# Gate and up projections as 15 products of three weight rows, two width halves and three token groups

## The chip, the core and the metric

The kernel runs on one core of a Trainium2 chip. The metric is device time in microseconds (us) from the start of the program to its end; lower is better. Five engines work side by side, each through its own queue in order: PE multiplies matrices, DVE and ACT work on tiles (both can read PE's result banks), POOL works on tiles that lie in SBUF, and SP here only issues transfers (DMAs) between DRAM and SBUF. An engine that waits for another holds up whatever stands behind the waiting instruction in its queue.

## What is computed

One layer of a decoder for 1024 prompt tokens and 32 sampled tokens, so 1056 in all, with a width of 1024 and a hidden width of 2816:

```python
def _layer(x, p, attn_fn, ...):
    h = _rms(x, n_mix_pre)
    z = h @ w_in
    ...
    mix = jnp.concatenate([a, m], axis=-1) @ w_out
    x = x + _rms(mix, n_mix_post)
    f = _rms(x, n_ffn_pre)
    f = (jax.nn.silu(f @ w_gate) * (f @ w_up)) @ w_down
    x = x + _rms(f, n_ffn_post)
    x = x + jax.nn.sigmoid(x @ w_ple_gate) * (p @ w_ple)
```

The change concerns `f @ w_gate`, `f @ w_up` and, for one third of the tokens, `@ w_down`.

## The kernel before

**Tokens and operands.** The 1056 tokens are three groups of N = 352 columns, numbered 0, 1, 2. Features lie on the 128 partitions. Every float32 operand of a matmul is kept as two parts, a rounded high part and the rest: `split` (L166) makes them with a copy on ACT and a subtraction on DVE. A product of 128 x 128 weights with 352 columns is then three matmuls (`gemm`, L412: high by high, high by low, low by high). A weight row of a block is 128 x 1024; over half of the width (four pieces of 128) a product costs 12 matmuls, over all of it 24.

**Gate and up.** The hidden width is 22 blocks of 128; each has a gate row and an up row. Groups 0 and 1 use a seven-product scheme: gate and up are two rows, the width has two halves (1 and 2), the groups are two columns, and the 2 x 2 x 2 product is made with seven half-width products instead of eight, from sums of weights and sums of operands (`T1` to `T4`, L1046). `w_sums` (L1122) forms the four weight sums with four POOL additions of 128 x 512, and splits them. Group 2 is done directly with the plain rows (`direct`, L1161). `gate_up` (L1151) runs one block: 7 x 12 + 2 x 24 = 132 matmuls. Its additions of product banks to SBUF tiles run on DVE.

**Order.** The blocks go in pairs, called slabs, 11 of them. `WALK` (L214) sets the order: first five slabs for group 2 alone, while the norms of groups 0 and 1 are still under way on the other engines, then all 11 for groups 0 and 1, six of them with group 2 as well. The down product of group 2 (`down`, L1215) is spread between the blocks: eight banks a slab, added to a running sum. PE's instructions stand in program order; those of the other engines are placed by a scheduler. `chain` and `turn` (L383) feed the steps of the norms (`ffn_steps`, L1002) in between, paced by a number of matmuls.

**Weights.** `need(k)` (L341) prepares the weights of item k and of up to four items behind it: it loads them into one of three raw buffers (`W_RAW`), and splits them into one of four pairs of buffers (`W_PAIRS`).

**Behind it.** The hidden rows of groups 0 and 1 and their differences are split at once (`stage`, L1082), written to DRAM with both parts (`spill`), and read back (`x_get`, L1259) for the down product in the same seven-product form (`down7`, L1271). Then the closing part (`ple_steps`, `ple_out`, `ple_first`, `ple_rest`) follows.

## Time and profile before

| | |
|---|---|
| three timed runs | 1077.48, 1078.29 (median), 1081.69 us |
| profiled execution | span 1076.7 us; no time of its own is listed beside it |
| HBM read, written | 123.02 MB, 37.86 MB |
| weight rows of gate and up read | 64 transfers of 512 KB |
| splits of plain weight rows (DVE, L168, `wl`) | 123, 162.9 us |
| weight sums on POOL (L1132, `wr`) | 47 + 46, 69.1 + 65.0 us |
| sums for the down stage on POOL (L339) | 44, 77.4 us |

In the profile's groups a row gives line, engine, operation, written tile <- read tiles, shapes, count; then busy time in us and the mean of one instruction in ns; then the idle time of the engine just ahead of them and what ended it. Names have their buffer numbers left out: `b` is a bank of PE's results, `wr` a raw weight row, `wh` and `wl` its two parts.

### The profile page before, as it was taken

The page shows a single profiled execution, that of the slowest core. Times are in us where ns is not written, and L with a number is a line of the kernel's source. Part 1 is how long each engine was busy: PE and PEld are TensorE (multiplying, and loading weights), DVE is VectorE, ACT ScalarE, POOL GpSimd, SP SyncE. Part 2 cuts the span into 40 slices and gives each one's busy share as a digit, 9 for nine tenths or more (in the row PEclk, how much of TensorE's full clock was granted, in tenths as well). Part 3 has the DMA queues.
Part 4 walks back from the last instruction along what each step waited for, and adds up shares of the span by engine and source line. Part 5 has one row for each costly group of instructions (what it writes and reads, how often), then busy time and mean ns, then how long its engine had stood idle before and what let it go on. Part 6 is the DMA issues. An engine that isn't in the chain of part 4 may idle for free.

```text
span 1076.7 us, 17467 instructions
## 1 busy us (share of the span) xinstructions
PE 1065.5 (99%) x6805; PEld 1049.6 (97%) x6805; DVE 828.7 (77%) x1229; ACT 525.7 (49%) x951; POOL 285.5 (27%) x213
## 2 busy tenths in 40 slices
PE   9999999999999999999999999999999999999997
PEld 8999988899999999999999999999999999999997
DVE  6766378977979957767758758659668877999898
ACT  8522277776855524344434434434344832476542
POOL 1045022200000032422324223232309076401170
PEclk9999999999999999999999999999999999999999
DMA  8121311352644312352441533614876955836422
GB/s 299 60 72 40 108 54 37 136 217 90 228 154 134 109 40 81 144 186 71 159 168 59 212 114 107 236 43 160 310 267 230 405 189 181 310 114 216 138 67 74
DMA packets 54162, 162.01 MB, mean 150 GB/s; under 512 B 5796, under 2 KB 20164, under 8 KB 54080
## 3 DMA queue, kind: packets, MB, share of 16 engines
q1 hardware_dynamic: 52752, 159.13, 42.2%
q10 hardware_dynamic: 1328, 1.77, 0.5%
q8 instruction: 53, 0.87, 0.4%
q14 instruction: 29, 0.24, 0.1%
HBM read 123.02 MB, written 37.86 MB: 149 GB/s over the span
## 4 chain that ended last, share of the span: by engine, by line
PE 91%; DVE 5%; ACT 2%; issue 1%; DMA 0%; ACTq 0%; SPq 0%; DVEq 0%
PE b L126 90%; DVE sl L168 1%; DVE sg L1439 1%; PE b L120 1%; DVE u L1286 1%; DVE ql L168 1%; DVE yo L1440 1%; DVE p L1476 0%; DMA xr<-in_x_dram 0%; ACT a L780 0%; DVE w L168 0%; DVE acc L930 0%; ACT qh L167 0%; DVE u L1476 0%; ACT sg L1436 0%
## 5 line engine op out<-in xcount | busy, mean ns | idle before, releaser
L126 PE MATMUL b<-fh,wh 128*128 128x352 f32 x720 | 231.4, 322 | 0.0
L126 PE MATMUL b<-fl,wh 128*128 128x352 f32 x716 | 229.3, 320 | 0.0
L126 PE MATMUL b<-fh,wl 128*128 128x352 f32 x716 | 229.2, 320 | 0.0
L1132 POOL TENSOR_TENSOR wr<-wr 128x512 f32<-128x512 f32 x47 | 69.1, 1470 | 538.1 <-DVE wl L168 512.4
L168 DVE TENSOR_TENSOR wl<-wr,wh 128x1024 fp32r<-128x1024 f32 (+1 forms) x123 | 162.9, 1326 | 51.3 <-ACT wh L167 51.2
L167 ACT CAST wh<-wr 128x1024 fp32r<-128x1024 f32 (+1 forms) x123 | 126.1, 1027 | 123.1 <-PE b L126 96.5
L126 PE MATMUL b<-xo,qh 128*128 128x352 f32 x620 | 147.7, 321 | 0.5 <-ACT u L1314 0.5
L126 PEld LDWEIGHTS b<-fh,wh 128*128 128x128 f32 x720 | 134.9, 188 | 0.0
L126 PE MATMUL b<-fh,sh 128*128 128x352 f32 x420 | 134.6, 322 | 0.0
L126 PEld LDWEIGHTS b<-fl,wh 128*128 128x128 f32 x716 | 134.5, 188 | 0.0
L126 PE MATMUL b<-fh,sl 128*128 128x352 f32 x416 | 133.2, 320 | 0.9 <-DVE sl L168 0.9
L126 PEld LDWEIGHTS b<-fh,wl 128*128 128x128 f32 x716 | 134.1, 187 | 0.0
L126 PE MATMUL b<-fl,sh 128*128 128x352 f32 x416 | 133.2, 320 | 0.0
L126 PE MATMUL b<-h,wh 128*128 128x352 f32 x480 | 112.6, 325 | 1.4 <-ACT h L504 1.2
L126 PEld LDWEIGHTS b<-xo,qh 128*128 128x128 f32 x620 | 107.1, 188 | 0.7 <-ACT u L1314 0.7
L126 PE MATMUL b<-xo,ql 128*128 128x352 f32 x308 | 99.1, 322 | 1.4 <-DVE ql L168 1.2
L339 POOL TENSOR_TENSOR wq<-wq,wq 128x512 f32<-128x512 f32 x44 | 77.4, 1797 | 66.0 <-DVE ql L168 56.3
L167 ACT CAST st<-c 128x352 fp32r<-128x352 f32 x55 | 26.8, 487 | 122.8 <-DVE c L1201 96.6
L126 PEld LDWEIGHTS b<-h,wh 128*128 128x128 f32 x480 | 83.3, 190 | 2.5 <-ACT h L504 1.4
L168 DVE TENSOR_TENSOR sl<-wr,sh 128x1024 fp32r<-128x1024 f32 x47 | 59.5, 1266 | 33.1 <-ACT sh L167 33.1
L126 PE MATMUL b<-hid,wh 128*128 128x352 f32 x352 | 84.0, 321 | 0.0
L126 PEld LDWEIGHTS b<-fh,sl 128*128 128x128 f32 x416 | 77.9, 187 | 1.2 <-DVE sl L168 1.2
(211 smaller groups left out, 2177.8 us busy)
## 6 DMA issues: line engine op xcount, KB each, us to landing
wr<-in_w_gu_dram SPq DMA_DIRECT2D x64, 512.0 KB, 3.4
xd<-st SPq DMA_DIRECT2D x35, 704.0 KB, 4.9
xo<-xd SPq DMA_DIRECT2D x35, 704.0 KB, 6.1
wr<-in_w_dn_dram SPq DMA_DIRECT2D x22, 512.0 KB, 4.2
wq<-in_w_dn_dram SPq DMA_DIRECT2D x20, 512.0 KB, 9.6
wr<-in_w_pg_dram SPq DMA_DIRECT2D x10, 512.0 KB, 3.5
x<-in_x_dram SPq DMA_DIRECT2D x6, 704.0 KB, 9.1
x1d<-x SPq DMA_DIRECT2D x6, 704.0 KB, 3.3
```

Of the source, the lines that this page charges most:

```text
L120: ins = te.transpose(out, src, ident)
L126: ins = te.matmul(*args, **kw)
L167: fix(se.copy(hi, src))
L168: fix(ve.tensor_tensor(lo, src, hi.bitcast(F32), op=ALU.subtract))
L339: ge.tensor_tensor(*(q_load(q, e)[:, i, :] for q in (out, a, b)), op=op)
L1132: ge.tensor_tensor(out, a, b, op=op)
L1286: ve.tensor_tensor(out, a, b, op=ALU.add)
L1439: ve.tensor_tensor(sg[:, v], sg[:, v], pp[:, v], op=ALU.mult)
L1440: ve.tensor_tensor(yo[:, v], sg[:, v], xm[:, v], op=ALU.add)
```

## The change

Gate and up use another scheme, with 15 half-width products for three weight rows, two halves and three groups, where the plain form has 18. The 44 rows form 14 triples (gate and up of one block, and one row of another) and a last pair with 11 products. Four of the 15 products of a triple need only the first two rows. They are made ahead, for all triples, in two passes (`two_ahead`), and written to DRAM (`p_d`), as are two half-row sums of weights (`s_d`). Then each triple loads both, and runs its 11 remaining products from six weight forms called 5, 3, 10, 8, 9 and 15 (`w_form`, `triple`). Form 9 is the last to read the first two rows. Some of the sums of pre-products run on POOL (`part_sums`). The hidden rows go to DRAM unsplit, half the bytes, and are split when they are read back (`x_get`, `hid_split`). The down product of group 2 becomes one block behind all triples (`down2`), with its eight banks held through it. Raw weight buffers are four instead of three.

```diff
-W_RAW = 3
+W_RAW = 4
+ROWS = 13
...
+    for t, rows in enumerate(TRIPLES):
+        FORM[t, "one"] = item("one", row_plan(*rows[0]), t)
+    for t, rows in enumerate(TRIPLES):
+        FORM[t, "two"] = item("two", row_plan(*rows[1]), t)
+    for t, rows in enumerate(TRIPLES):
+        jr = [row_plan(*r) for r in rows]
+        js = add_plan(s_d[t], [P, KC, P])
+        in_a.add(js)
+        FORM[t, "5"] = item("5", *jr[:2])
+        FORM[t, "3"] = item("3", js, *jr[:2])
+        FORM[t, "10"] = item("10", js, *jr[2:])
+        if len(rows) > 2:
+            FORM[t, "8"] = item("8", jr[2])
+        FORM[t, "9"] = item("9", *jr)
+        if len(rows) > 2:
+            FORM[t, "15"] = item("15", js, jr[2])
...
+        if kind in ("one", "two"):
+            r = raws[js[0]]
+            at = slice(4, 8) if kind == "one" else slice(0, 4)
+            add(r[:, at, :], r[:, 0:4, :], r[:, 4:8, :])
+            nc.sync.dma_start(s_d[js[1]][:, at, :], r[:, at, :])
+            hl = w_tile([P, KC, P], "fh"), w_tile([P, KC, P], "fl")
+            split(*hl, r)
+            return hl
...
+        if kind == "5":
+            r0, r1 = r
+            add(r0[:, one, :], r0[:, one, :], r1[:, two, :], sub)
+            split(*hl, r0[:, one, :])
+        elif kind == "3":
+            s, r0, r1 = r
+            add(r0[:, one, :], r0[:, one, :], s[:, one, :])
+            add(r1[:, two, :], r0[:, two, :], r1[:, two, :])
+            halves(r0[:, one, :], r1[:, two, :])
+        elif kind == "10":
+            if len(r) > 1:
+                add(r[0], r[0], r[1])
+            split(*hl, r[0])
+        elif kind == "8":
+            split(*hl, r[0])
+        elif kind == "9":
+            if len(r) > 2:
+                add(r[1][:, one, :], r[1][:, one, :], r[2][:, one, :])
+                add(r[0][:, two, :], r[0][:, two, :], r[2][:, two, :])
+            halves(r[1][:, one, :], r[0][:, two, :])
+        else:
+            s, r2 = r
+            add(s[:, one, :], s[:, one, :], r2[:, two, :])
+            add(s[:, two, :], s[:, two, :], r2[:, one, :])
+            split(*hl, s)
...
+    def two_ahead(t, i):
+
+        w = need(FORM[t, ("one", "two")[i]])
+        st = act_tile([P, 2, N], s="st")
+        for h, key in enumerate((("X1", "B23"), ("B11", "X4"))[i]):
+            at = 1 - h if i else h
+            se.copy(st[:, at, :], product(w, h, key)[:, :N])
+        nc.sync.dma_start(p_d[t][:, 2 * i : 2 * i + 2, :], st)
...
+    def part_load(t):
+        if t < NT:
+            parts[t] = [act_tile([P, 4, N], s="p")]
+            nc.sync.dma_start(parts[t][0], p_d[t])
+
+    def part_sums(t):
+        if t < NT:
+            p = parts[t][0]
+            q = act_tile([P, 4, N], s="q")
+            parts[t].append(q)
+            ge.tensor_tensor(q[:, 0:2, :], p[:, 0:2, :], p[:, 1:3, :], op=ALU.add)
+            ge.tensor_tensor(q[:, 2, :], p[:, 0, :], p[:, 3, :], op=ALU.add)
+            ge.tensor_tensor(q[:, 3, :], p[:, 2, :], p[:, 3, :], op=ALU.add)
...
+        part_load(t + 1)
+        b5 = product(need(FORM[t, "5"]), None, "X5")
+        tt(q2, b5[:, :N], q2)
+        w3 = need(FORM[t, "3"])
+        b3 = product(w3, 0, "X3")
+        tt(q2, b3[:, :N], q2, sub)
+        w = need(FORM[t, "10"])
+        b10 = product(w, 0, "X10")
+        if full:
+            tt(p3, b10[:, :N], p3)
+        b13 = product(w, 1, "X13")
+        if full:
+            tt(p1, b13[:, :N], p1)
+        product(w3, 1, "X6", b5)
+        tt(q1, b5[:, :N], q1, sub)
+        se.activation(q[:, 0:2, :], q[:, 0:2, :], AF.Silu)
+        if full:
+            w = need(FORM[t, "8"])
+            b8 = product(w, 0, "B12")
+            c32 = tmp(N, "c32")
+            se.copy(c32, b8[:, :N])
+            tt(p2, b8[:, :N], p2)
+            b11 = product(w, 1, "B22")
+            tt(p0, b11[:, :N], p0)
+            tt(c32, b11[:, :N], c32)
+        part_sums(t + 1)
+        tt(q[:, 0:2, :], q[:, 0:2, :], q[:, 2:4, :], ALU.mult)
+        w = need(FORM[t, "9"])
+        product(w, 0, "X9", b10)
+        tt(p2, b10[:, :N], p2, sub)
+        product(w, 1, "X12", b13)
+        tt(p0, b13[:, :N], p0, sub)
+        h1 = tmp(N, "h1")
+        se.activation(h1, p0, AF.Silu)
+        tt(h1, h1, p2, ALU.mult)
+        c = rows[0][0]
+        chunk_put(c, q1, h1, q0)
++        if not full:
             return
+        w = need(FORM[t, "15"])
+        product(w, 0, "X15", b11)
+        minus(p3, b11, p3)
+        product(w, 1, "X14", b8)
+        minus(p1, b8, p1)
...
+    def down2():
+
+        os_[2] = [half(2, s="o") for h in range(2)]
+        banks = [bank() for _ in range(KC)]
+        for s in range(NSLAB):
+            hid_get(s + 2)
+            if s >= NSLAB - 2:
+                x_get(s - NSLAB + 2)
+            h = hid.pop(s)
+            for m in range(KC):
+                wh, wl = need(WD[s][m // 4])
+                if m == 2:
+                    hid_split(s + 1)
...
-                    nc.sync.dma_start(t[:, :, :w].bitcast(F32), spilled[key, e][:, :, :w])
+                    raw = t[:, 1, :w].bitcast(F32)
+                    nc.sync.dma_start(raw, spilled[key, e][:, :w])
+                    split(t[:, 0, :w], t[:, 1, :w], raw)
...
+    for t in range(NT):
+        two_ahead(t, 0)
+    for t in range(NT):
+        two_ahead(t, 1)
+        if t == NT - 2:
+            part_load(0)
+        if t == NT - 1:
+            part_sums(0)
+    for t in range(NT):
+        triple(t)
+        if t == NT - 2:
+            hid_get(0)
+        if t == NT - 1:
+            hid_get(1)
+            hid_split(0)
+    down2()
```

What this does to the engines' queues is seen in the order of the built program. First POOL, in the middle of gate and up. Before, two blocks in a row (`wr` with a number is one raw weight row, each row is written and read in place):

```order
L1132 TENSOR_TENSOR wr784_4943<-wr784_4943 128x512
L1132 TENSOR_TENSOR wr784_4943<-wr757_4728,wr784_4943 128x512
L1132 TENSOR_TENSOR wr757_4728<-wr784_4943,wr757_4728 128x512
L1132 TENSOR_TENSOR wr757_4728<-wr757_4728 128x512
L1132 TENSOR_TENSOR wr810_5135<-wr810_5135 128x512
L1132 TENSOR_TENSOR wr810_5135<-wr789_4953,wr810_5135 128x512
```

And now, one triple with the sums for the next (`wr816`, `wr817`, `wr825` are its three rows, `a821` the stored half sums, `p844` and `q864` the next triple's pre-products and their sums):

```order
L342 TENSOR_TENSOR wr816_4765<-wr816_4765,wr817_4767 128x512
L342 TENSOR_TENSOR wr817_4767<-wr816_4765,wr817_4767 128x512
L342 TENSOR_TENSOR wr817_4767<-wr817_4767,wr825_4810 128x512
L342 TENSOR_TENSOR wr816_4765<-wr816_4765,wr825_4810 128x512
L342 TENSOR_TENSOR wr816_4765<-wr816_4765,a821_4789 128x512
L342 TENSOR_TENSOR a821_4789<-a821_4789,wr825_4810 128x1024
L342 TENSOR_TENSOR a821_4789<-a821_4789,wr825_4810 128x512 x2
L1243 TENSOR_TENSOR q864_5117<-p844_4979 128x704
L1244 TENSOR_TENSOR q864_5117<-p844_4979 128x352
L1245 TENSOR_TENSOR q864_5117<-p844_4979 128x352
```

Where four additions stood to a block, there are now eleven instructions to a triple: the adds of forms 5, 3, 9, 9, 3, 10 and 15, then the three sums.

Second DVE, in the triple ahead of that one (its tiles are `p779`, `q799`, `c32831`). The rows begin with the split of its form 9 and run to the additions behind the split of the next triple's form 3 (`b` is a bank; `fw` are the parts of a weight form):

```order
L164 TENSOR_TENSOR fw815_4758<-wr782_4534,fw814_4757 128x512
L1258 TENSOR_TENSOR q799_4662<-b818_4769,q799_4662 128x352
L1258 TENSOR_TENSOR q799_4662<-b822_4791,q799_4662 128x352
L1258 TENSOR_TENSOR p779_4524<-b826_4812,p779_4524 128x352
L1258 TENSOR_TENSOR p779_4524<-b827_4826,p779_4524 128x352
L164 TENSOR_TENSOR fw820_4784<-a787_4558,fw819_4783 128x1024
L1258 TENSOR_TENSOR q799_4662<-b818_4769,q799_4662 128x352
L164 TENSOR_TENSOR fw824_4806<-wr816_4765,fw823_4805 128x512
L1258 TENSOR_TENSOR q799_4662<-q799_4662 128x704
L1258 TENSOR_TENSOR p779_4524<-b830_4862,p779_4524 128x352
L1258 TENSOR_TENSOR p779_4524<-b832_4878,p779_4524 128x352
L164 TENSOR_TENSOR fw829_4855<-wr816_4765,fw828_4854 128x512
```

Right behind these come:

```order
L164 TENSOR_TENSOR fw829_4855<-wr817_4767,fw828_4854 128x512
L1258 TENSOR_TENSOR c32831_4875<-b832_4878,c32831_4875 128x352
L1258 TENSOR_TENSOR p779_4524<-b826_4812,p779_4524 128x352
L1258 TENSOR_TENSOR p779_4524<-b827_4826,p779_4524 128x352
L164 TENSOR_TENSOR fw835_4899<-a821_4789,fw834_4898 128x1024
```

The splits of the next triple's forms 5 and 3 (`fw824`, `fw829`) stand ahead of this triple's addition to `c32831` from bank `b832`, the bank that product X15 accumulates onto. Before, the same stretch of DVE's queue, one block, read

```order
L1167 TENSOR_TENSOR c21882_5578<-u3880_5563,b873_5490 128x352
L1201 TENSOR_TENSOR c21882_5578<-c21882_5578,c11874_5503 128x352
L1167 TENSOR_TENSOR u3880_5563<-u3880_5563,b883_5581 128x352
L1167 TENSOR_TENSOR p1861_5451<-p1861_5451,b883_5581 128x352
L168 TENSOR_TENSOR st827_5257<-c21882_5578,st827_5257 128x352
L168 TENSOR_TENSOR sl896_5696<-wr848_5345,sh895_5695 128x1024
L1167 TENSOR_TENSOR p1861_5451<-p1861_5451,b884_5596 128x352
```

with two splits of sums to a block and no later block's split between a bank and its reader.

Third SP, the transfers' queue, now (`h`, `t1`, `t2`, `t4` are hidden rows and their differences, stored as `xd`):

```order
L1157 DMA xd808_4712<-t4838_4936 128x352
L175 DMA a852_5013<-sd28_107 128x1024
L175 DMA wr848_4991<-in_w_gu_dram 128x1024
L175 DMA wr856_5034<-in_w_gu_dram 128x1024
L175 DMA wr883_5222<-in_w_gu_dram 128x1024
L1236 DMA p880_5212<-pd14_93 128x1408
```

The second and third row of a triple (`wr848`, `wr856`) are loaded behind the last stores of the triple two before it, and ahead of the first row of the next one (`wr883`) and of its pre-products (`p880`).

More of the change, by code (lines that the diff above doesn't have):

```diff
@@ L381, in trunk_kernel, with step @@
     share = [0.6]
+    def step(ch):
+        try:
+            load, wait = next(ch[0])
+        except StopIteration:
+            chains.remove(ch)
+            return
+        dve[0] = max(dve[0], now[0]) + load / share[0]
+        ch[1] = dve[0] + wait
     def turn(n):
@@ L1065, in trunk_kernel @@
         out_proj(m, 0)
-    chain(ffn_steps(0), 19)
+    chain(ffn_steps(0), 19, alone=True)
     for m in range(4, KC):
```

342 lines of the change are left out of this document (150 added, 192 removed).

## The prediction

> **What bounds the kernel now.** I read the head of the page first: which engine is busy, and how the chain of work that ended last divides.
>
> ```profile
> span 1076.7 us, 17467 instructions
> PE 1065.5 (99%) x6805; PEld 1049.6 (97%) x6805; DVE 828.7 (77%) x1229; ACT 525.7 (49%) x951; POOL 285.5 (27%) x213
> PE 91%; DVE 5%; ACT 2%; issue 1%; DMA 0%; ACTq 0%; SPq 0%; DVEq 0%
> ```
>
> PE is busy for 99% of the span and is 91% of the chain. That says little of each stage, so next I read the chain in order of time and the table by stretches of 50 us (columns: stretch, its length, then busy time and count of PE, PEld, DVE, ACT and POOL, granted clock, DMA share, GB/s).
>
> ```profile
> 208.20 618.03 PE b L126 x3894
> 300.00:350.00 50.00, 50.00 (x316) 50.00 (x316) 43.36 (x65) 26.32 (x35) 0.00 (x0) 1.00 0.44 140
> 450.00:500.00 50.00, 50.00 (x316) 50.00 (x315) 31.03 (x49) 18.03 (x28) 17.11 (x12) 1.00 0.31 115
> 800.00:850.00 50.00, 49.52 (x312) 49.26 (x312) 41.69 (x43) 31.73 (x52) 27.65 (x16) 1.00 0.80 309
> ```
>
> From 208 to 826 us, which is all of gate and up, PE runs without a gap: 50 us hold 316 matmuls, 0.158 us each at clock 1.00. So a matmul taken out there is worth 0.158 us, provided that everything feeding PE keeps pace. POOL is the quiet engine there: 17.11 us in 50.
>
> **What is removed.** Before, a column block costs seven products of 12 matmuls for groups 0 and 1 and two direct products of 24 for group 2: 132, times 22 blocks is 2904. After, 14 triples of 15 products and one of 11 make 221 products of 12: 2652. The down product of group 2 keeps its 528 matmuls, and two short spacers go. 252 x 0.158 = **39.8 us off**. The order of the built program agrees that nothing else of PE changes.
>
> **What feeding a product costs now.** These rows price it.
>
> ```profile
> L168 DVE TENSOR_TENSOR wl<-wr,wh 128x1024 fp32r<-128x1024 f32 (+1 forms) x123 | 162.9, 1326 | 51.3 <-ACT wh L167 51.2
> L1167 DVE TENSOR_TENSOR p<-p,b 128x352 f32<-128x352 f32 x66 | 33.8, 512 | 0.0
> L1132 POOL TENSOR_TENSOR wr<-wr,wr 128x512 f32<-128x512 f32 x46 | 65.0, 1414 | 3.6
> L167 ACT CAST qh<-wq x42: 602/1050/1070, 801.6 to 948.1; 128x1024 fp32r<-128x1024 f32 x35, 128x512 fp32r<-128x512 f32 x7
> L168 DVE TENSOR_TENSOR ql<-wq,qh x42: 678/1226/2318, 802.8 to 953.3; 128x1024 fp32r<-128x1024 f32 x35, 128x512 fp32r<-128x512 f32 x7
> wr<-in_w_gu_dram SPq DMA_DIRECT2D x64, 512.0 KB, 3.4
> ```
>
> One 1024-column split is 1.05 us on ACT and 1.23 on DVE; half of one is 0.60 and 0.68; a 512-column add on POOL about 1.4; a weight row lands 3.4 us after its issue. DVE's maximum of 2.318 beside a median of 1.226 asks for a look at single instructions, in a stretch where POOL is busy too (columns: start, duration, engine, line, form).
>
> ```profile
> 865.46 1.23 DVE L168 TENSOR_TENSOR ql<-wq,qh 128x1024 fp32r<-128x1024 f32 x1 [2.40 <-ACT qh L167]
> 866.77 1.30 POOL L339 TENSOR_TENSOR wq<-wq,wq 128x512 f32<-128x512 f32 x1 [29.65 <-DVE ql L168]
> 871.61 2.68 DVE L168 TENSOR_TENSOR fl<-x,fh 128x1408 fp32r<-128x1408 f32 x1
> 872.76 2.68 POOL L339 TENSOR_TENSOR wq<-wq,wq 128x512 f32<-128x512 f32 x1
> 874.21 0.51 DVE L1286 TENSOR_TENSOR u<-u,b 128x352 f32<-128x352 f32 x1
> 874.64 1.88 DVE L168 TENSOR_TENSOR ql<-wq,qh 128x1024 fp32r<-128x1024 f32 x1
> ```
>
> The ends tell it. DVE's split ends at 874.29; POOL's add, begun at 872.76, ends at 875.44, 1.15 later; DVE's next split, begun at 874.64, ends at 876.52, 1.08 later. They take turns: a DVE instruction that reads two SBUF tiles and a POOL add **do not overlap**, and each is charged with the other. DVE's add that reads a PSUM bank (874.21, 0.51) passes freely.
>
> Now the sum of turns in one triple, whose 11 products take 132 x 0.158 = 20.9 us on PE. POOL has seven adds of 512 columns, one of 1024, and sums of 704, 352 and 352. With 1.15 for 512 and, as an estimate scaled from it, 2.1, 1.5 and 0.86 twice: 13.4 us. DVE has 5.5 full splits at 1.08 (5.9), one multiply of 704 columns (0.75) and 5.5 instructions of 352 (0.38 each, scaled): 8.8 us. Together **22.2 us against PE's 20.9**, so even perfectly packed turns lose 1.3 us per triple. Before, four adds stood against a column block of 132 matmuls, and nothing here was close.
>
> **The loop that ties one triple to the next.** The four raw buffers hold three rows and the next triple's first; the second row of the next triple is loaded only when form 9 of this triple has been split. I follow it from the end of product X5, at 1.9 us of the triple. Form 9: two half casts and the last subtraction, 1.9, ends at 3.8. Load, 3.4: 7.2. Five POOL adds in a row (forms 5, 3, 9, 9, 3) at 1.4: 14.2. Two half casts and a subtraction of form 3: 16.1. Behind these splits DVE has the addition to c32, which reads the bank that product X15 will accumulate onto, 0.5: 16.6. PE wants that bank after nine products, at 17.1. The margin is **0.5 us with nobody in the way**. In the way are:
> - ahead of form 9's split: two adds of form 15 and the three sums on POOL (5.5 us of turns), with 2 to 4 us of DVE's own, so that the split ends at 6 to 8 and not at 3.8;
> - between the five adds: the splits of 15 and 5 and the multiply, 2.4 us of turns;
> - behind the fifth add: form 10's add of 1024 columns begins before the cast of form 3 is ready and holds the two subtractions up, 1 to 1.5 us.
>
> That is 5.6 to 8.1 us for a margin of 0.5, so at worst 7.6 us of PE per triple; at best the packed turns, 1.3 us. Nothing below that: the turns are in the rows. I take the middle, **4.5 us**, because PSUM reads fill part of DVE's waiting. Thirteen triples have a successor: 13 x 4.5 = **58.5 us** (17 to 99).
>
> The c32 addition stands behind the splits because of DVE's order; queued behind it are the evictions of X9 and X12, form 10's split and the Silu's multiply, so a late row delays all of the next triple's start. The SP queue adds to it rather than relieving it: the load of that row stands behind the stores of the block before, which wait for DVE's last differences, and ahead of the part products' load.
>
> **The rest, with its cover.** The 30 pre-products take 60 x 1.9 = 114 us of PE. Turns there: 30 adds and three sums of 1408 columns on POOL (43 us), 30 splits (32 us) and about 30 instructions of 1408 columns plus small ones of the two norm chains (53 us, 1.5 each by the one that ends at 874.29): 128 us, of which some run ahead of the stage. The splits run up to four forms ahead, 11 us of cover. Zero to 15 us; I take **5**. Its transfers, per pre-product pair a weight row in, half a row and two part products out, 1.15 MB per 3.8 us or 302 GB/s, stay under the 309 GB/s at which the 800:850 row still has PE at 49.52 of 50. The group-2 down block costs nothing: one split per 24 matmuls, 1.23 us of DVE and less than an add of cover for 3.8 us of PE, and no POOL work.
>
> ```profile
> xo<-xd SPq DMA_DIRECT2D x35, 704.0 KB, 6.1
> xo<-xd SPq DMA_DIRECT2D x7, 352.0 KB, 5.0
> L168 DVE TENSOR_TENSOR st<-c,st 128x352 fp32r<-128x352 f32 x55 | 31.3, 568 | 6.7 <-ACT st L167 6.1
> ```
>
> In the seven-product down stage the hidden rows now arrive whole and are split on arrival: the 154 staged splits of the gate stage go, which no step of PE waited for, and 42 splits come in here. A step of 48 matmuls is 7.6 us; the load took 6.1 and fitted. A half-size load takes about 5.0, then 0.75 on ACT and 0.75 on DVE, a second one behind it, and turns with 44 POOL adds: 6.5 to 8.5. Zero to 1 us on some 16 steps; I take **5** (0 to 15). The two borders of the triples, where two rows have to come in at once and where the last bank drains: 2 (0 to 4).
>
> **The sum.** 1076.7 - 39.8 + 58.5 + 5 + 5 + 2 = 1107.4 of span. No separate time is given for the profiled execution; the median of the three runs, 1078.29, lies 1.6 above its span, and I add that: **1109 us**, slower by 2.8%.
>
> **Rivals.**
> 1. *The turns pack well and PE stays the bound (faster).* If the scheduler's order lets POOL's sums fall into DVE's PSUM reads, the loss is the packed 1.3 us per triple plus little: 1076.7 - 39.8 + 17 + 4 + 1.6 = 1060. For it: PSUM reads pass freely, and 12 of a triple's DVE instructions are such. It decides as long as a triple's stall stays under 2.3 us, where 13 stalls eat what is left of 39.8 after some 10 us elsewhere. Against it: a margin of 0.5 us in the loop. Chance 22%.
> 2. *The stalls are long enough to slow PE's clock.* The table by stretches of 4 us at the start shows it:
>
> ```profile
> 8.00:12.00 4.00, 4.00 (x17) 3.83 (x15) 2.96 (x7) 2.75 (x6) 0.00 (x0) 0.57 1.05 369
> 12.00:16.00 4.00, 4.00 (x27) 4.00 (x26) 3.77 (x9) 3.55 (x8) 0.00 (x0) 1.00 1.06 401
> ```
>
>    After a start with gaps the granted clock is 0.57 for a while and 17 matmuls run instead of 27, a loss of about 1.6 us. If each of 13 stalls did that: 13 x 1.6 = 21, to 1130. Against it: past the start the trace has no gap of 4 us, so nothing says that one such gap is enough. Chance 17%. The Trainium skill, "TensorE: Matmul & The Clock Gate", "What's actually happening", has the clock halve after an idle window of about 3.4 us that runs freely: by it gaps of 4.5 us would be punished only sometimes, so it stands between the two sums, and gaps under 3.4 us would cost nothing.
> 3. *Break-even*, a stall of 2.3 to 3.2: 1073 to 1084. Chance 9%.
> 4. *The transfers bind in the pre-product stage.* At 280 GB/s instead of 309 an item's 1.15 MB would take 4.1 us and not 3.8, 30 x 0.3 = 9 more. That lies inside my range for that stage and is no case of its own.
> 5. *The change removes fewer matmuls than it says*: the count of the built program rules it out.
>
> **Chances and range.** My forecast, stalls of about 3.2 to 6.5 us: 1084 to 1128, 48%; rival 2, 1128 to 1150, 17%; rival 1, 1050 to 1073, 22%; break-even 9%; the rest beyond. The range 1053 to 1143 leaves out under 2 in 10. Half a percent (about 5.4 us) is what a measurement of this kernel can tell from no change: faster 0.23, same 0.08, slower 0.69.
>
> **What would show it.** PE: about 254 matmuls fewer. In the triples: PE gaps once per triple, ahead of the matmul that accumulates X15, released by DVE's c32 addition; DVE splits of 1024 columns at well over 1.3 us on average there; POOL adds near 2 us; POOL waiting for a weight row's DMA. If instead PE is at 50 of 50 in those stretches, the loop has slack that I missed and rival 1 holds. If the gaps are elsewhere (in the pre-products, or in the down stage behind the hidden rows' casts), my terms are mis-sized.

## The result, and the profile after

The changed kernel takes **1175.2 us** (median of 4 runs, 1175.06 to 1176.22) against 1078.88 for the kernel before in the same comparison: a ratio of 1.0895, 95% interval [1.0876, 1.0914]. It is slower, as forecast, but by 96 us and not by 31, and outside the range.

The head of the page of the changed kernel, its busy times and how its chain divides:

```profile
span 1174.4 us, 17444 instructions
PE 1070.9 (91%) x6551; PEld 1040.8 (89%) x6551; DVE 943.1 (80%) x1179; ACT 547.8 (47%) x984; POOL 495.4 (42%) x318
PE 55%; POOL 13%; issue 12%; DVE 10%; DMA 5%; ACT 4%; SPq 0%; ACTq 0%; POOLq 0%; DVEq 0%
```

PE has 254 matmuls fewer, as the change says, and is no longer nearly all of the chain: 45% of it now lies elsewhere, the largest part on POOL (13%). Where the time went shows in the table by stretches, cut at the first matmul of each stage (columns: stretch, its length, busy time and count of PE, PEld, DVE, ACT, POOL, granted clock, DMA share, GB/s). First the kernel before, gate, up and group 2's down together, then its seven-product down stage:

```profile
263.80:810.70 546.90, 546.90 (x3444) 546.90 (x3444) 409.31 (x598) 241.90 (x355) 125.13 (x89) 1.00 0.43 149
810.70:961.90 151.20, 149.35 (x935) 148.41 (x934) 126.84 (x131) 76.86 (x122) 76.18 (x44) 1.00 0.70 248
```

And the changed kernel: the wait ahead of the first pre-product, the pre-products, the first two triples, the other triples, group 2's down, the seven-product stage:

```profile
264.50:271.30 6.80, 0.33 (x3) 0.04 (x1) 6.80 (x6) 4.49 (x5) 1.64 (x2) 0.86 0.58 210
271.30:402.20 130.90, 121.87 (x726) 120.06 (x727) 111.38 (x81) 67.59 (x106) 60.86 (x31) 0.96 0.73 250
402.20:472.00 69.80, 50.31 (x267) 47.27 (x266) 57.38 (x57) 27.69 (x39) 52.59 (x31) 0.90 0.41 137
472.00:796.60 324.60, 283.22 (x1670) 278.89 (x1669) 277.71 (x339) 109.69 (x164) 208.49 (x127) 0.95 0.50 167
796.60:881.60 85.00, 85.00 (x530) 85.00 (x529) 36.93 (x37) 31.65 (x38) 1.29 (x2) 1.00 0.70 241
881.60:1057.00 175.40, 158.66 (x935) 153.71 (x935) 156.09 (x161) 101.12 (x160) 80.87 (x43) 0.97 0.39 125
```

Against 0.158 us for each matmul of the program: the wait ahead loses 7 us, the pre-products (720 matmuls, 113.8) 17, the first two triples (264, 41.7) 28, the other triples (1668, 263.5) 61, and the seven-product stage takes 24 more than before. That is 137. Less the 40 us of removed matmuls it is about the 98 by which the spans differ.

The groups of the page that price the turns now (DVE's half splits of weight forms, POOL's adds of two rows; 0.68 and 1.41 us before):

```profile
L164 DVE TENSOR_TENSOR fw<-wr,fw 128x512 fp32r<-128x512 f32 x89 | 126.1, 1443 | 35.8 <-ACT fw L163 35.6
L342 POOL TENSOR_TENSOR wr<-wr,wr 128x512 f32<-128x512 f32 x58 | 98.3, 1713 | 22.4 <-DMA wr<-in_w_gu_dram 21.1
```

Both are slower, as the forecast looked for. Its own marks were splits of 1024 columns at well over 1.3 us, which took 1.49 us (29 of them) and 1.34 us (14) in the triples, and adds near 2 us, which took 1.7. What PE waited for, over the whole span (engine, line, what for: us in total, times, longest):

```profile
PE b L125 <- DVE c L1258: 45.5, 13, 6.6
PE b L125 <- DVE xo L164: 8.8, 9, 4.5
PE b L125 <- DVE q L1258: 8.5, 7, 2.1
PE b L125 <- DVE fl L164: 7.6, 5, 2.3
PE b L125 <- ACT fh L163: 6.6, 1, 6.6
```

The first row is the wait that was forecast, DVE's addition to c32 ahead of product X15, 13 times (`c` in the row). Two of the 13 lie in the first two triples, 11.5 us, and eleven in the other triples, 33.9 us; there a long one of 3.6 to 4.3 us and a short one of 1.8 to 2.4 us take turns from triple to triple, for a reason that no run here shows. The last row is the wait ahead of the first pre-product. One wait for c32, in the order of time (start, duration, engine, line, form):

```profile
537.35 3.65 POOL L342 TENSOR_TENSOR wr<-wr,wr 128x512 f32<-128x512 f32 x2
540.96 1.29 POOL L342 TENSOR_TENSOR wr<-wr,a 128x512 f32<-128x512 f32 x1
542.33 2.35 POOL L342 TENSOR_TENSOR a<-a,wr 128x1024 f32<-128x1024 f32 x1
542.94 2.89 DVE L164 TENSOR_TENSOR fw<-wr,fw 128x512 fp32r<-128x512 f32 x2 [2.23 <-ACT fw L163]
545.75 0.51 DVE L1258 TENSOR_TENSOR c<-b,c 128x352 f32<-128x352 f32 x1
```

The fifth add ends at 542.25; form 10's add of 1024 columns runs until 544.68 and holds up form 3's two subtractions, which take 2.89 us; behind them comes c32, and PE goes on at 546.3. PE's clock around this gap:

```profile
542.50:546.30 3.80, 0.33 (x3) 0.04 (x1) 3.36 (x4) 1.97 (x3) 2.18 (x1) 0.95 0.00 0
546.30:549.70 3.40, 3.29 (x12) 3.32 (x13) 2.39 (x4) 0.50 (x1) 1.36 (x1) 0.56 0.02 5
549.70:553.00 3.30, 3.30 (x23) 3.30 (x22) 2.20 (x4) 2.13 (x4) 1.38 (x2) 1.00 0.21 62
```

After 3.8 us of waiting PE does 12 matmuls in 3.4 us and not 22: the gap costs nearly half as much again. In the trace's record of the clock the changed kernel has 70.8 us at half clock, in 16 stretches, and the kernel before 9.1. PE was at work in 57.6 and 3.4 us of these, so the lower clock cost some 27 us more than before, half of the difference; this is contained in the stages above. Within the triples it is 44.4 us at half clock, 38.3 of them with PE at work, a loss of some 19.

### The profile page after: what moved, and what is told of

Read it like the earlier page. It is cut to its first block, busy times and chain, and to the rows that moved or that the text cites. A ratio compares the mean times of both kernels' runs of the same rounds, so it can differ in the third digit from the quotient of the medians.

```text
span 1174.4 us, 17444 instructions
## 1 busy us (share of the span) xinstructions
PE 1070.9 (91%) x6551; PEld 1040.8 (89%) x6551; DVE 943.1 (80%) x1179; ACT 547.8 (47%) x984; POOL 495.4 (42%) x318
## 3 DMA queue, kind: packets, MB, share of 16 engines
q10 hardware_dynamic: 1328, 1.77, 0.5%
## 4 chain that ended last, share of the span: by engine, by line
PE 55%; POOL 13%; issue 12%; DVE 10%; DMA 5%; ACT 4%; SPq 0%; ACTq 0%; POOLq 0%; DVEq 0%
PE b L125 54%; POOL wr L342 8%; DMA wr<-in_w_gu_dram 3%; POOL a L342 2%; DVE u L1410 2%; DVE xo L164 2%; DVE ql L164 1%; POOL q L1244 1%; DVE fl L164 1%; DVE fw L164 1%; POOL q L1245 1%; POOL q L1243 1%; ACT fw L163 1%; DMA xo<-xd 1%; PE b L119 1%
## 5 line engine op out<-in xcount | busy, mean ns | idle before, releaser
L125 PE MATMUL b<-fh,fw 128*128 128x352 f32 x1288 | 329.1, 336 | 60.9 <-DVE c L1258 45.5
L125 PEld LDWEIGHTS b<-fh,fw 128*128 128x128 f32 x1288 | 235.8, 197 | 68.2 <-ACT fw L163 46.7
L125 PE MATMUL b<-fl,fw 128*128 128x352 f32 x644 | 214.1, 332 | 0.0
L125 PE MATMUL b<-xo,qh 128*128 128x352 f32 x620 | 154.5, 330 | 10.3 <-DVE xo L164 8.8
L164 DVE TENSOR_TENSOR fw<-wr,fw 128x512 fp32r<-128x512 f32 x89 | 126.1, 1443 | 35.8 <-ACT fw L163 35.6
L125 PEld LDWEIGHTS b<-fl,fw 128*128 128x128 f32 x644 | 128.1, 199 | 0.0
L164 DVE TENSOR_TENSOR wl<-wr,wh 128x1024 fp32r<-128x1024 f32 (+1 forms) x59 | 73.6, 1251 | 44.3 <-ACT wh L163 44.0
L342 POOL TENSOR_TENSOR wr<-wr,wr 128x512 f32<-128x512 f32 x58 | 98.3, 1713 | 22.4 <-DMA wr<-in_w_gu_dram 21.1
L342 POOL TENSOR_TENSOR a<-a,wr 128x512 f32<-128x512 f32 (+1 forms) x42 | 74.7, 1791 | 50.8 <-DVE fw L164 49.7
L125 PE MATMUL b<-fh,fh 128*128 128x352 f32 x240 | 79.5, 331 | 6.6 <-ACT fh L163 6.6
L125 PE MATMUL b<-fh,fl 128*128 128x352 f32 x240 | 79.4, 331 | 5.4 <-DVE fl L164 5.4
L125 PE MATMUL b<-fl,fh 128*128 128x352 f32 x240 | 78.8, 328 | 2.1 <-DVE fl L164 2.1
```

Source lines behind the costliest of these rows:

```text
L125: ins = te.matmul(*args, **kw)
L164: fix(ve.tensor_tensor(lo, src, hi.bitcast(F32), op=ALU.subtract))
L342: ge.tensor_tensor(out, a, b, op=op)
```

## The experiments

Each is the changed kernel with one edit, timed once, unless said otherwise. Stages are measured from first matmul to first matmul; "triples" were 394.4 us in the changed kernel.

### Is it the one wait?

**Banks of their own for X15 and X14**, and **forms made three ahead instead of four** (so that c32 stands ahead of form 3's subtractions):

```diff
+            minus(p3, b11, p3)
+            minus(p1, b8, p1)
...
-        product(w, 0, "X15", b11)
-        minus(p3, b11, p3)
-        product(w, 1, "X14", b8)
-        minus(p1, b8, p1)
+        less(p3, product(w, 0, "X15"))
+        less(p1, product(w, 1, "X14"))
```

(`less(out, ps)` is `out - ps`; what X15 and X14 were added onto is now subtracted ahead of them, which is two DVE instructions more per triple.) The second edit gives every `need` of a triple a 3:

```diff
-        w3 = need(FORM[t, "3"])
+        w3 = need(FORM[t, "3"], 3)
```

> Products X15 and X14 get banks of their own; what they were added onto is subtracted by VectorE in two instructions more per triple. Theory A (a wait for one bank: X15 cannot begin until VectorE's c32 addition, which stands behind the splits of the next triple's second form): the 45.5 us of PE's waiting for c32 go to nearly nothing, nothing of like size takes their place, the triples' stage falls from 394 us to 320 to 345, most of the stretches at half clock go with the gaps, and the kernel takes about 1105 to 1125 us. Theory B (VectorE's and GpSimd's instructions take turns, and their sum per triple, 25 to 26 us, binds): the wait moves to another bank or to a weight split, the stage stays at 380 to 395 us, the kernel at 1165 to 1180.

> In the triples the weight forms are made three ahead instead of four, which puts VectorE's c32 addition ahead of the two subtractions of the next triple's second form, and changes no work at all. Theory A (the place in VectorE's queue makes the wait): c32 waits under 10 us in all, triples' stage 320 to 350 us, kernel 1105 to 1130 us. Theory B (the turns bind): PE then waits for the forms themselves, the stage stays at 380 us or more, the kernel at 1165 or more; being one form less ahead could even cost 5 to 10 us.

Measured: 1171.6 and 1156.4 us. With own banks, the triples' stretch:

```profile
408.00:794.30 386.30, 329.03 (x1934) 323.79 (x1934) 344.70 (x420) 135.65 (x202) 264.56 (x157) 0.92 0.48 163
```

And PE's two longest waits:

```profile
PE b L125 <- DVE q L1258: 42.4, 7, 7.6
PE b L125 <- DVE fw L164: 12.1, 7, 3.3
```

The c32 wait is gone and a wait for q, the bank of X6, has 42.4 us in its place. Three ahead:

```profile
401.70:777.40 375.70, 328.03 (x1934) 320.90 (x1933) 338.06 (x393) 134.80 (x203) 269.88 (x157) 0.96 0.50 168
```

There c32 still has 12.3 us of PE's waiting and the additions into q, from other banks, 24.5. So theory A, which put the stage at 320 to 350 us, falls: c32 is where the delay comes out, not where it arises. The order of DVE's queue is worth 19 us. Theory B had 380 us or more and a kernel of 1165 or more for the second edit, and missed that as well.

### Is it the loop, GpSimd's round, or the sum of the work?

**Part sums on VectorE** (`ge` becomes `ve` in the three additions of `part_sums`), and **form 15 in a buffer of its own**:

```diff
-            add(s[:, one, :], s[:, one, :], r2[:, two, :])
-            add(s[:, two, :], s[:, two, :], r2[:, one, :])
-            split(*hl, s)
+            n = act_tile([P, KC, P], s="s15")
+            add(n[:, one, :], s[:, one, :], r2[:, two, :])
+            add(n[:, two, :], s[:, two, :], r2[:, one, :])
+            split(*hl, n)
```

> The three part sums of a triple go from GpSimd to VectorE. Theory C (GpSimd's queue is one round per triple, about 26 us in the changed kernel: some 20 us of adds, of which the part sums are 5, and 6 of waiting in order for VectorE's split of form 10, for the Silus and for the row's load; PE is paced by that round): the round falls to about 21 us, the triples' stage from 394 us to 330 to 350, the kernel to 1115 to 1135. Theory B (the sum of VectorE's and GpSimd's turns): 5 us off GpSimd, 2 onto VectorE, so the stage falls to 350 to 370. Theory D (the load of the next triple's second row sets the round): the sums lie in that load's shadow, and the stage stays at 380 to 400.

> Form 15 is added into a buffer of its own and no longer over form 10, so that GpSimd needn't wait until VectorE has split form 10 (49.7 us of GpSimd's waiting in 13 places in the triples' stage). No work is added or removed. Theory C (GpSimd's round in order): the round loses up to 4 us, the triples' stage falls from 394 us to 345 to 375, the kernel to 1125 to 1155. Theory B (turns) and D (row load): the sum of work and the loads are the same, the stage stays at 385 to 400, the kernel at 1166 to 1180.

Measured: 1167.4 us with triples of 388.1, and 1186.3 us with triples of 408.2, slower than the changed kernel. Theory C expected 330 to 350 in the first and 345 to 375 in the second. With the sums gone from POOL, it waits for the row instead, 115.1 us in the triples where the changed kernel has 14.5:

```profile
POOL wr L342 <- DMA wr<-in_w_gu_dram: 115.1, 18, 10.4
```

The sums lay in the load's shadow, as theory D had it; theory B's 350 to 370 was missed too. In the other kernel the wait was not removed but exchanged for a longer one: the slot of the new buffer is held until DVE has made the differences of the hidden rows, and POOL waits for those, 88.1 us instead of 49.7:

```profile
POOL s L342 <- DVE t L1170: 88.1, 13, 7.6
```

So it tests theory C less cleanly than it was meant to.

**Five raw buffers** (`W_RAW = 5`, `ROWS = 10`), alone and with forms three ahead:

> Five raw buffers for weight rows instead of four (and ten small row tiles instead of thirteen, which pays for the fifth), so that the next triple's second row is loaded without waiting for this triple's form 9 to be split; the third row now waits for that. No other work changes. Theory L (the loop that the prediction drew: split of form 9, load of the row, five adds on GpSimd, splits of form 3, what stands behind them in VectorE's queue; its length, not the engines' work, sets the period of 26 us): the triples' stage falls from 394 us to 325 to 350, the kernel to 1105 to 1131. Theory B (VectorE's and GpSimd's turns fill the period): the stage stays at 375 us or more, the kernel at 1156 or more.

> Five raw buffers and forms made three ahead, together. Three ahead alone gave 376 us for the triples. Theory L: both shorten the same loop, the stage is at 315 to 340 us and the kernel at 1095 to 1121. Theory B: 365 to 380 us, no better than three ahead alone, kernel 1145 to 1160.

Measured: 1161.0 and 1153.1 us.

```profile
400.90:780.10 379.20, 326.95 (x1933) 320.29 (x1932) 336.09 (x393) 138.05 (x202) 265.12 (x157) 0.95 0.50 168
```

```profile
400.70:773.90 373.20, 327.74 (x1934) 321.09 (x1933) 342.75 (x394) 135.58 (x203) 274.19 (x158) 0.95 0.51 174
```

So these two edits of the loop are worth 15 and 21 us of the 89 that the triples lost; with five buffers the third row still waits for form 9, so the loop isn't gone. From start and length of every instruction in the traces I worked out how long, within the triples, a POOL add or a DVE instruction on two SBUF tiles ran: some 350 us in the changed kernel and as much, within 3 us, with own banks, three ahead, five buffers and both. An instruction that waits for its turn counts as running there, so this is not a bound that is shown: with the part sums on DVE it is 335 us, and that stage fell by 6 us only, to 388.

### The turns by themselves

**Thin adds**: the adds of the weight forms and of the down stage's quarters on an eighth of their columns, so that most columns of these weights stay unsummed.

```diff
-            ge.tensor_tensor(out, a, b, op=op)
+            ge.tensor_tensor(*(t[:, :, 0:16] for t in (out, a, b)), op=op)
...
-            ge.tensor_tensor(*(q_load(q, e)[:, i, :] for q in (out, a, b)), op=op)
+            ge.tensor_tensor(*(q_load(q, e)[:, i, 0:64] for q in (out, a, b)), op=op)
```

> GpSimd's adds of the weight forms and of the down stage's quarters are done on an eighth of their columns only (so those weights are left mostly unsummed); every load, split, matmul and wait stays. Triples: theories B and C (GpSimd's adds, by turns or by its round) both put the stage at 306 to 330 us; theory D (the row's load) keeps it above 360. Seven-product down stage, 175 us: if VectorE's own work binds there (the 42 splits on arrival came on top of 128 us), it stays above 163; if the splits and GpSimd's sums hold each other up, it falls to 149 to 158. A median of VectorE's 1024-column split of 1.23 us, against a mean above 1.4 before, would show the turns alone.

**Spare adds**, and **spare fills**, both on top of the thin adds (and hidden rows two steps ahead); `scrap` is a tile of 512 columns that nothing else reads, `c` in the rows:

```diff
                 add(r[0], r[0], r[1])
+                for _ in range(8):
+                    ge.tensor_tensor(scrap, scrap, r[0][:, 0:4, :], op=ALU.add)
```

```diff
                 add(r[0], r[0], r[1])
+                add(scrap, scrap, r[0][:, 0:4, :])
+                for _ in range(24):
+                    ge.memset(scrap, 0.0)
```

> GpSimd's adds on an eighth of their columns as before (that kernel: triples 323.6 us, seven-product stage 161.2), and behind form 10's add eight spare adds of 512 columns per triple, which nobody waits for: GpSimd is as busy as in the changed kernel and takes as many turns, but the adds that the loop waits for stay short. Theory L: the triples' stage stays at 320 to 335 us. Theory B: VectorE's splits are held up by the spare adds, and the stage goes back to 365 us or more. In between, the two share it in that proportion. In the seven-product stage, with the quarters' sums thin, hidden rows are fetched two steps ahead: if lateness of the rows and turns with the sums were two separate losses there, it falls from 161 us to 149 to 154; if they were one, it stays at 158 to 162.

> The kernel with thin adds again, but the spare work behind form 10's add is 24 fills of 512 columns, which write a tile and read none, about 12 us per triple by the one fill of 1152 columns (1.06 us) in the trace of before: GpSimd is about as busy as with the eight spare adds (301 us of 375 there, triples 382 us). Theory B (turns between instructions that read two tiles on VectorE and GpSimd's adds): fills aren't in the way, VectorE's 1024-column split of form 15 stays near 1.24 us, the triples' stage at 320 to 335 us. Theory C (GpSimd's own round in order, whatever it does): the stage is back at 365 us or more with VectorE's splits not slowed. A stage over 365 with slow splits would say that fills take turns as well, and leave it open.

Measured: 1078.7, 1128.1 and 1089.9 us. The triples with thin adds:

```profile
388.90:712.30 323.40, 314.48 (x1934) 310.95 (x1933) 270.25 (x394) 137.53 (x204) 131.34 (x158) 0.98 0.58 199
```

The group of DVE's half splits in it:

```profile
L164 DVE TENSOR_TENSOR fw<-wr,fw 128x512 fp32r<-128x512 f32 x75 | 73.7, 1014 | 10.1 <-ACT fw L163 9.8
```

With the spare adds:

```profile
389.40:771.30 381.90, 333.00 (x1934) 326.93 (x1934) 345.26 (x393) 136.63 (x204) 306.27 (x267) 0.93 0.48 166
```

The spare adds and the half splits among the groups:

```profile
L377 POOL TENSOR_TENSOR c<-c,a 128x512 f32<-128x512 f32 x112 | 177.1, 1581 | 8.8
L164 DVE TENSOR_TENSOR fw<-wr,fw 128x512 fp32r<-128x512 f32 x75 | 97.3, 1328 | 12.0 <-ACT fw L163 11.8
```

With the spare fills:

```profile
390.50:733.40 342.90, 317.50 (x1934) 313.02 (x1933) 246.69 (x393) 135.79 (x204) 291.12 (x507) 0.98 0.53 185
```

The fills and the half splits:

```profile
L378 POOL MEMSET c<- 128x512 f32 x336 | 176.7, 526 | 17.5
L164 DVE TENSOR_TENSOR fw<-wr,fw 128x512 fp32r<-128x512 f32 x75 | 53.3, 743 | 52.7 <-ACT fw L163 52.6
```

Theory D had the stage above 360 us with thin adds, since the load stays; 323 rules it out as the whole cause. Adds and fills keep POOL busy for the same 177 us. Beside the fills DVE's half split takes 743 ns and the stage 343 us, which is outside both expected ranges, nearer to theory B's 320 to 335 than to theory C's 365 or more; beside the adds, which nobody waits for either, it is 1328 ns and 382 us. DVE does the same work in 247 us there and in 345 here. So the ladder for the triples is: 305 for the matmuls; 323 with thin adds (18 us that no step here takes apart); 343 when POOL is busy without reading (its round in order, 20 us); 382 when it reads as well (turns with DVE, 39 us); 394 when the loop waits for these adds (12 us). Of the 39, PE's waiting is some 24 and the lower clock behind it some 14. The steps come from different kernels, and POOL is somewhat busier with the spare adds than in the changed kernel, so the turns' share is at the high end. Theory B carries the largest part, C and L a part each.

### The other stages

**Pre-products with B23 ahead of X1 and hidden rows two steps ahead**; **stores off SP's queue**; **three B23 first and the long sums apart**:

```diff
-        for h, key in enumerate((("X1", "B23"), ("B11", "X4"))[i]):
+        for h, key in (((1, "B23"), (0, "X1")), ((0, "B11"), (1, "X4")))[i]:
...
-        for i in range(n, n + 2):
+        for i in range(n, n + 3):
```

```diff
-        nc.sync.dma_start(p_d[t][:, 2 * i : 2 * i + 2, :], st)
+        nc.scalar.dma_start(p_d[t][:, 2 * i : 2 * i + 2, :], st)
...
-            nc.sync.dma_start(s_d[js[1]][:, at, :], r[:, at, :])
+            nc.gpsimd.dma_start(s_d[js[1]][:, at, :], r[:, at, :])
```

```diff
-    for t in range(NT):
-        two_ahead(t, 0)
+    for hs in ((1,), (0,)):
+        for t in range(3):
+            two_ahead(t, 0, hs)
+    for t in range(3, NT):
+        two_ahead(t, 0)
...
+                early_x[key] = b_sum(None, a, b, eng=ge)
+                yield 0, 40
```

> Two edits in two stages far apart. First: of each first pair of pre-products, the one with B23 (ready first) comes ahead of the one with X1. If the gap of 12.5 us ahead of the pre-products is the wait for X1's difference and split, it falls to 7 to 9 us; if it is the norm chain of group 2 itself, it stays above 11. Second: in the seven-product down stage the hidden rows are fetched two steps ahead instead of one. If the wait there is for load plus split started too late, the stage falls from 175 us to 150 to 158; if the splits and the sums on GpSimd hold each other up, it stays above 168. Both right: about 1147 to 1153 us; both wrong: 1173 to 1177.

> In the pre-products the part products are stored from ScalarE's queue and the weight sums from GpSimd's, so that no load of a weight row on SyncE's queue stands behind a store that waits. If that order makes the rows late, the pre-products' stage falls from 131 us to 116 to 122 and the kernel to about 1160 to 1167; if VectorE's and GpSimd's turns hold the stage, it stays at 127 to 133 and the kernel at 1170 to 1178. The triples' stage is not touched: 390 to 398 in either case.

> Two edits ahead of the triples. The first three pre-products with B23 run ahead of the first with X1, so that 5.7 us of PE's work stand in the wait for X1. And GpSimd's three sums of 1408 columns, which stood in a row for 12 us ahead of the weight rows' adds, stand apart, with adds between. If these two are what the entry and the pre-products lost, the last pre-product ends at 386 to 394 us instead of 402, the gaps of 1.6 and 2.5 us at 337 and 343 us are gone, and the kernel takes 1160 to 1168 us. If the weight rows' loads or the splits hold the stage, it ends at 399 or later, and the kernel stays at 1171 to 1177.

Measured: 1171.5, 1171.0 and 1171.6 us. In the first, PE began at 265.3 and then waited for X1 all the same, 4.5 us; its pre-products end at 401.7 as before: that edit gains nothing. Off SP's queue the stage is 128.6 us, a small gain and not the cause; 116 to 122 would have made it one. The third kernel, its pre-products, then its triples, then the first of these:

```profile
265.30:387.20 121.90, 118.49 (x728) 117.39 (x727) 109.05 (x79) 65.50 (x105) 58.28 (x30) 0.99 0.80 278
387.20:792.70 405.50, 334.52 (x1934) 328.16 (x1933) 346.10 (x402) 143.84 (x209) 269.38 (x159) 0.92 0.46 158
387.20:442.80 55.60, 27.19 (x134) 25.29 (x134) 51.69 (x38) 26.15 (x33) 43.52 (x21) 0.75 0.32 114
```

The pre-products end at 387.2, 15 us earlier, as expected; but the kernel is only 3.6 us faster, where 1160 to 1168 was expected, since the first triple then takes 55.6 us for 132 matmuls, with DVE busy for 51.7 of them. DVE has not finished group 1's operands, and PE waits 27 us there for their two parts (12.5 for the casts, 14.8 for the subtractions): what is won ahead of them is waited for behind. The seven-product stage with hidden rows two steps ahead, with thin sums, and with both:

```profile
882.50:1049.60 167.10, 153.97 (x935) 151.46 (x934) 160.68 (x159) 100.11 (x158) 80.94 (x44) 0.98 0.38 123
```

```profile
796.20:957.40 161.20, 154.14 (x935) 152.53 (x935) 127.30 (x161) 101.18 (x160) 22.77 (x40) 0.98 0.43 136
```

```profile
855.20:1007.30 152.10, 149.53 (x935) 148.13 (x934) 125.14 (x159) 99.89 (x158) 23.85 (x40) 1.00 0.42 136
```

From 175.4 us the one takes 8 and the other 14, and both together bring it to 152.1, next to the 151.2 of before: two separate losses, rows that come a step late, and 42 more splits that take turns with POOL's sums. DVE's work by itself, 125 us of 152, has room.

### All of it together, and the clock

**Five buffers, three ahead, part sums on VectorE, hidden rows two steps ahead, the pre-products' edits**; and the same **with own banks**:

> All edits together that took something off: five raw buffers, forms three ahead, the part sums on VectorE, hidden rows fetched two steps ahead, three pre-products with B23 first and GpSimd's long sums apart. With five raw buffers and three ahead, the time in which GpSimd or one of VectorE's two-tile instructions ran was 350 us of a stage of 373. Theory B (turns): the part sums take 4.5 us off GpSimd and put some 2.3 onto VectorE per triple, so that time falls to about 320 us and the stage to 335 to 355; seven-product stage about 167; together 1105 to 1128 us. Theory L (only the waits counted): the stage is at 306 to 325 and the kernel at 1075 to 1100. Neither is below the kernel before by more than can be measured.

> As the kernel with all edits, and banks of their own for X15 and X14. Theory B: GpSimd's and VectorE's turns bind, so the two more VectorE instructions per triple that read a bank neither help nor cost: within 8 us of the kernel with all edits. Theory L: a wait less, 10 to 25 us below it.

Measured: 1134.5 us (4 runs, 1133.3 to 1136.2), ratio to the kernel before 1.0526 [1.0508, 1.0543], and 1133.8 us. The first triple and the last ones of the first kernel:

```profile
387.40:439.80 52.40, 25.52 (x134) 24.33 (x133) 49.42 (x43) 24.00 (x29) 28.48 (x14) 0.74 0.32 109
461.10:761.30 300.20, 278.69 (x1670) 273.67 (x1669) 278.84 (x378) 107.90 (x165) 157.88 (x91) 0.97 0.52 180
```

In the first triple PE waited for operands of group 1 (`fh` and `fl` there):

```profile
PE b L125 <- DVE fl L164: 15.5, 2, 8.3
PE b L125 <- ACT fh L163: 11.3, 2, 10.9
```

From the third triple on it takes 300 us and not 325. The stage as a whole, 373.9, misses its 335 to 355, and the kernel its 1105 to 1128, in the main because the first triple waits as above: it is 31 us over its matmuls. Own banks add nothing. No version here beats the kernel before. The kernel with thin adds is the nearest, level with it at 1078.7: even with most of the sums left out, what remains eats all that the removed matmuls bring.

**Twelve matmuls more ahead of X15**, into a bank that nobody reads:

```diff
+        w9 = w
...
+        keep_on = bank()
+        for k in range(4):
+            for _ in range(3):
+                mm(keep_on[:, :N], w9[0][:, 4 + k, :], operand("X12")[0][:, k, :], start=True, stop=True)
         product(w, 0, "X15", b11)
```

> In each triple, ahead of product X15, TensorE runs 12 matmuls more, on operands that it has and into a bank that nobody reads: 1.9 us of work in the place where it waits for the c32 addition. If the granted clock falls because of gaps of some 3.5 us and more (each gap of 3.7 to 6.7 us in the triples of the changed kernel was followed by a stretch at half clock, of those under 2.6 us few), the gaps of 3.7 to 4.5 us fall to 1.8 to 2.6, half the stretches at half clock in the triples go, and though TensorE has 168 matmuls more, the stage falls from 394 us to 378 to 390. If the clock follows something else, or the round of VectorE and GpSimd is all that counts, it stays at 392 to 400; if the 12 matmuls stand in the way, 400 to 420.

Measured: 1181.1 us, triples 403.3, and 79.8 us at half clock in the whole run. The stage is in the range expected for matmuls that stand in the way. The 168 matmuls are 26.5 us of work; the waits for c32 fell by 14 us, to 31.8 in 11 places, but the gaps in every other triple were as long as before (3.4 to 5.0 us). So the long gaps were not shortened, and the clock's share by itself was not tested.

## Why the prediction was wrong

- **Removed matmuls, 39.8:** right; 254 fewer, and where nothing waits they run at 0.158 us.
- **The triples, 58.5 (13 stalls of 4.5):** right in place, and near in size by luck. The c32 wait came 13 times, but at 3.5 us each, 45.5 in all. Eleven of the 13 lie from the third triple on, where the forecast has 49.5 us and the stage lost 61: 33.9 for c32, 7.5 for another bank, the rest for the most part the clock. The reason given, a loop with a margin of 0.5 us lengthened by turns, weighed the two the wrong way round: the edits put 12 to 21 us on the loop and up to 39 on the turns. "Together 22.2 us against PE's 20.9" was too low, since 1.15 and 1.08 came from one place where instructions queued closely; the add at 866.77 among the same rows, which began ahead of DVE's next split, took 1.30. Measured as above, turns are some 350 us over 14 triples and the short one, or 23.9 for 132 matmuls, with a POOL add at 1.7 us.
- **The borders, "2 (0 to 4)": a step that failed.** The first two triples lost 28 us, where two stalls (9) and this term make 11. "Where two rows have to come in at once" counted a load, not that every form of the first triple starts from nothing there while DVE still has operands of group 1 to make (six splits, 10.3 of its 29.0 us in the first triple). PE's waits were 11.5 us for c32, 6.6 for weight forms and 1.1 for a bank, and 13.7 us were at half clock; how much of this the operands caused was not tested in this kernel. The wait of 7 us ahead of the first pre-product had no term at all; it is X1, which needs both halves of group 2, where the kernel before began with one.
- **The pre-products, "I take 5" (0 to 15): a step that failed.** They lost 17, though the forecast's own count, 128 us of turns against 114 of PE, was 14 over. Three long POOL sums stood in a row ahead of the adds of the rows; taking them apart, with B23 first, in one edit, ended the stage 15 us earlier, though DVE took most of that back later.
- **The seven-product stage, "I take 5" (0 to 15): the largest miss of a single term.** It lost 24. Both mechanisms had been named, the half-size load a step late and the turns; each step's price was put at 0 to 1 us, and it was 1.5. Fetching two steps ahead and thin sums took off 8 and 14, and both 23.
- **Rival 2, the clock:** it was not a rival. It came on top of the waits, and the sum had it at nothing. Its price, 21 us for 13 stalls, is near the 19 that the clock lost in the triples; over the whole kernel it lost 27. It was these losses behind stalls shorter than the forecast's 4.5 that brought the triples up to size.

By the numbers, the forecast was 66 us short: some 12 in the later triples, 17 in the first two, 12 in the pre-products, 19 in the seven-product stage and 7 ahead of the pre-products. The sum took the middle of a range for the triples' stalls but 5 of 15 for each of two stages; it had no term for the entry and none for the clock, and took no account of all these stages being fed by the same DVE.

The prediction had the clock, by the Trainium skill, "TensorE: Matmul & The Clock Gate", "What's actually happening", spare some gaps of 4.5 us, since its window runs freely. The trace decides otherwise: all eight gaps of 3.7 to 6.7 us in the triples were followed by half clock, and so were three of nine between 1.9 and 2.6 us, which the prediction's reading had at no cost.

## What to carry to other kernels

A change that trades matmuls for additions is priced, stage by stage, by the time of all VectorE instructions on two SBUF tiles plus all GpSimd adds, against the matmuls of the same period, at the durations that they have beside each other; in the versions here that sum everything it came to 335 us or more in the triples against PE's 305, and no buffer and no order that was tried brought the gain back. Price the seams, the first round of each stage, with what must be made before it, and not by an average of later rounds. And each stall of PE of 3.7 us or more was followed here by half clock, which over the eight cost about half as much again, so that goes into the sum, not among the rivals.

## What the runs showed of the hardware

- GpSimd's fills and adds are not alike for VectorE. At equal GpSimd time (176.7 and 177.1 us) a split of 512 columns took 743 ns beside fills and 1328 beside adds. The Trainium skill, "SBUF — State Buffer", "Who interferes with whom", has VectorE instructions with two SBUF inputs contend with GpSimd's reads and not with its writes alone; these runs agree.
- The granted clock followed PE's gaps closely. In the triples of the changed kernel eight of eight gaps of 3.7 us or more were followed by one or two stretches of 3.4 us at half clock, and of nine gaps of 1.9 to 2.6 us three, two of these next to each other ahead of one stretch. A gap is counted here from the start of the last matmul ahead of it to the start of the next. The row 619.9 to 622.5, a gap of 2.55 us, left the clock as it was:

```profile
619.90:622.50 2.60, 0.31 (x2) 0.02 (x1) 2.60 (x4) 1.05 (x1) 0.96 (x1) 1.00 0.00 0
622.50:626.00 3.50, 3.41 (x21) 3.44 (x22) 3.50 (x7) 0.50 (x1) 1.04 (x1) 1.00 0.17 56
```
